# Split weights kept in DRAM after the first block, position rows read from DRAM on ACT's queue: a decoder layer on one Trainium2 core

## The chip, the cores and the metric

The kernel runs on one core of a Trainium2 chip. The metric is the device time of one launch in microseconds (us), lower is better. Its engines are TensorE (PE, with its weight loads shown apart as PEld), VectorE (DVE), ScalarE (ACT), GpSimd (POOL) and SyncE (SP), which only issues transfers here. SP and ACT each have a queue of their own for DMA transfers; both queues share the core's 16 DMA engines.

## What is computed

One decoder layer over 2048 tokens with a model width of 1024, all in float32. A combined projection feeds two branches, a gated DeltaNet (4 heads of 128) and a sliding-window attention (8 query heads of 64, 2 key/value heads, window 128) with a relative-position bias, which are gated and merged; a SwiGLU block with 2816 hidden columns follows.

```python
h = rms_norm(x, attn_norm[l])
proj = h @ w_in[l]
dn_qkv, dn_z, dn_b, dn_a, sq, sk, sv, gate_raw = split_combined(proj)
y_dn = gated_deltanet_branch(dn_qkv, dn_z, dn_b, dn_a, ...)
y_swa = sliding_window_branch(sq, sk, sv, q_gain, k_gain, sinks, rel_bias)
gates = sigmoid(gate_raw).reshape(B, S, 2, D_MODEL)
merged = gates[:, :, 0] * (y_dn @ w_branch_dn[l]) + gates[:, :, 1] * (y_swa @ w_branch_swa[l])
x = x + merged @ w_out[l]
h2 = rms_norm(x, ffn_norm[l])
x = x + (silu(h2 @ w_gate[l]) * (h2 @ w_up[l])) @ w_down[l]
```

In the attention branch `logits = where(mask, q k^T + bias, -inf)`, where `bias[head, i, j]` is a value of `rel_bias` (32 buckets by 8 heads) chosen by the distance between the query and the key.

## The kernel before

**Tiling.** The 2048 tokens are worked on in four blocks of 512. Each block goes through the same stages: the projections of keys and values (skv) and queries (sq), the DeltaNet projections and heads (dn) among which the attention tiles are spread, the branch gates (g), the branch outputs (br), their merge, the output product (wo), the norm, and the FFN in five parts of up and down products. The window products (skv, sq) of the next block are done before the FFN of this one.

**Weights.** They lie in DRAM as 120 units: two for skv (128 x 1056 values) and 118 others (128 x 1024, 512 KB each). Every block uses every unit once, so there are 480 loads. `weights()` (L151) loads a unit on SP's queue into `wraw` (three buffers) and splits it in two halves j = 0, 1. ACT copies the half to `whi`, rounded to the matmul's format fp32r; DVE and POOL in turn subtract (`wlo` = `wraw` - `whi`). `whi` and `wlo` have four half buffers each (HB). A product is then three matmuls (`mm3`, `tok_mm`): hi by hi, hi by the lo of the other operand, lo by hi. One unit is 24 matmuls of 512 columns. In `chan_gemm` (per-channel products: dn, g, br, up) the first half serves the first 12 of them and the second half the rest; in `tok_gemm` (wo, down) and in sq both halves are used in turn until the unit ends.

**Position bias.** `band_bias()` (L279) is a side task at the start of block 0. It loads the table and a one-hot matrix, multiplies them on PE (oh by rb), copies the 8 x 384 result to `tab`, and then needs, for each head, 128 rows that are each shifted by one against the last (`bt`). Eight transfers on SP's queue read them from the one SBUF partition that holds the head's row, 128 overlapping pieces of 1 KB each. Four pairs of heads are then flipped by a matmul with `anti` and copied to `bias`.

**Order.** PE runs in the order in which the program writes it. `drive()` (L193) mixes the dense products with side tasks (norms, attention tiles, DeltaNet heads, the bias): each side task says by its `yield` when it wants to go on, and an estimate of the engines' times (`Estimate`, L56) decides when it does. `weights()` uses the raw engine handles, so the estimate doesn't see the loads and the splits. The other engines run in an order that the scheduler sets from dependencies and priorities; side tasks have a higher priority. A queue's transfers and an engine's instructions start in their order; one that waits holds those behind it.

**Names.** `x` is a 128 x 512 half tile of the input; `xn` or the scaled `x` its normed form, `st` the norm's statistics, `h` the transposed pair (hi, lo). `kr`, `ksq`, `kst`, `kn` are steps of the key norm, `ba` the columns for beta and decay. `G` are the gates and then the merged branch, `mt` their split form. `be`, `bm`, `bl`, `bc`, `bch` and `B` belong to the DeltaNet heads. `acc` and `aux` are PSUM tiles. L108 in the rows is a line of a helper through which nearly every instruction passes.

Of the kernel before, what the change touches and what calls it, by code (L numbers as in the profile page):

```python
# [8 lines left out]
F32 = mybir.dt.float32  # L9
F32R = mybir.dt.float32r  # L10
I32 = mybir.dt.int32
AF = mybir.ActivationFunctionType
ALU = mybir.AluOpType
AX = mybir.AxisListType

P = 128
# [7 lines left out]
NQ = 8  # L24
# [3 lines left out]
FSPLIT = (4, 4, 4, 4, 6)  # L28
NU = 63
ND = 6  # L30
HB = 4
PSUB = 2
LANES = 2
GATES_AT = 2
# [18 lines left out]
UNITS = {k: i for i, k in enumerate(KEYS)}  # L53


class Estimate:  # L56


    def __init__(self):
        self.now = 0.0  # L60
        self.done = 0.0
        self.free = {}
        self.ready = {}
        self.banks = {}
        self.seq = 0
# [48 lines left out]
class Emitter:  # L114
    def __init__(self, ctx, tc, ins, out, nblocks):
        self.tc, self.raw, self.out = tc, tc.nc, out
        self.est = Estimate()
        self.nc = Noted(tc.nc, self.est)
        self.__dict__.update(ins)
        self.nblocks = nblocks  # L120
        pool = lambda name, bufs, **kw: ctx.enter_context(tc.tile_pool(name=name, bufs=bufs, **kw))
        self.cp = pool("const", 1)
        self.tp = pool("tiny", 2)
        self.wp = pool("w", 3)
        self.up = pool("u", NU)
        self.dp = pool("d", ND)
        self.bp = pool("b", 1)
        self.pacc = pool("acc", 8, space=bass.MemoryType.PSUM)
        self.nsub = 0

# [20 lines left out]
    def weights(self, key, a):  # L151
        nc = self.raw
        n = a * 264 if key[0] == "skv" else 1024
        src = self.w_skv[key[1]] if key[0] == "skv" else self.w_all[UNITS[key]]
        raw = self.wp.tile([P, 1056], F32, name="wraw", tag="wraw")
        nc.sync.dma_start(out=raw[:, :n], in_=src)
        hl = []
        for j in range(2):
            hi = self.wp.tile([P, 528], F32R, name="whi", tag="whi", bufs=HB)
            lo = self.wp.tile([P, 528], F32R, name="wlo", tag="wlo", bufs=HB)  # L160
            r = raw[:, j * n // 2:(j + 1) * n // 2]
            nc.scalar.activation(hi[:, :n // 2], r, AF.Copy)  # L162
            self.nsub += 1
            eng = nc.vector if self.nsub > 6 and self.nsub % PSUB else nc.gpsimd
            eng.tensor_tensor(out=lo[:, :n // 2], in0=r, in1=hi[:, :n // 2], op=ALU.subtract)  # L165
            hl.append([t[:, :n // 2].rearrange("p (a m) -> p a m", a=a // 2) for t in (hi, lo)])
        h = a // 2
        return lambda k: (hl[k // h][0][:, k % h], hl[k // h][1][:, k % h])

    def mm3(self, ps, lh, ll, rh, rl, first, last):  # L170
# [108 lines left out]
    def band_bias(self):  # L279

        nc = self.nc
        yield 20000
        rb = self.u([8], name="rb")
        nc.sync.dma_start(out=rb[0:33, :], in_=self.rel_bias)
        oh = self.u([384], name="oh")
        nc.sync.dma_start(out=oh[0:33, :], in_=self.onehot)
        anti = self.u([P], name="anti")
        nc.sync.dma_start(out=anti, in_=self.flip)
        yield 8000
        ps = self.aux()  # L290
        nc.tensor.matmul(ps[0:8, 0:384], rb[0:33, :], oh[0:33, :], start=True, stop=True)
        tab = self.u([384], name="tab")
        nc.vector.tensor_copy(out=tab[0:8, :], in_=ps[0:8, 0:384])
        bt = [self.u([2, 2 * P], name="bt") for _ in range(4)]
        for h in range(NQ):
            row = tab[h:h + 1, :]
            src = bass.AP(tensor=row.tensor, offset=row.offset, ap=[list(row.ap[0]), [1, P], [1, 2 * P]])
            nc.sync.dma_start(out=bt[h // 2][:, h % 2, :], in_=src)
        yield 0
        yield 14000  # L300
        for i in range(4):
            ps = self.aux()
            nc.tensor.matmul(ps, anti, bt[i], start=True, stop=True)
            nc.scalar.activation(self.bias[:, 2 * i:2 * i + 2, :], ps, AF.Copy)
            yield 0
        self.bias_ready = True
# [775 lines left out]
```

## Time and profile before

| | us |
|---|---|
| median of 3 runs | 3273.05 (3271.22 to 3273.44) |
| the profiled execution, its own time | 3272.67 |
| its span, first to last instruction | 3270.9 |
| PE busy | 3122.2 (95% of the span) |
| DVE busy | 1752.7 (54%) |
| ACT busy | 1262.6 (39%) |
| POOL busy | 896.7 (27%) |

The mean granted clock of PE is 0.982 of full speed. The four blocks end at roughly 930, 1733, 2536 and 3271 us. Of the engines other than PE, ACT spends 604.0 us and POOL 640.5 us on splitting weights, DVE 356.4. The transfers move 281.27 MB, a mean of 86 GB/s.

A row of the timeline gives the start, the duration, the engine, the line, the operation, its output and inputs, and how many alike stand in a row; in square brackets stands how long the engine sat idle before it and which instruction released it.

### The profile page before, as it was taken

The numbers are of one execution on the slowest core, as the hardware profiler recorded it, in microseconds if no ns is written. First come the engines' busy times: TensorE is split into PE (matmuls) and PEld (weight loads), VectorE is DVE, ScalarE is ACT, GpSimd is POOL, SyncE is SP. The second block draws the span as 40 slices with busy tenths as digits, with TensorE's granted clock in tenths as the row PEclk, the third lists the DMA queues.
The fourth block names the chain that finished last, engine by engine and source line by source line (L and its number), as shares of the span: only waits on it lengthen the run. The fifth ranks groups of instructions, "written<-read, shape, count | busy, mean of one in ns | idle before, by whom it ended". The sixth has DMA issues, their size and how long they took to land. (4 is left out here: it accounts for less than half of the span.)

```text
span 3270.9 us, 40889 instructions
## 1 busy us (share of the span) xinstructions
PE 3122.2 (95%) x14854; PEld 2536.8 (78%) x14854; DVE 1752.7 (54%) x3986; ACT 1262.6 (39%) x2832; POOL 896.7 (27%) x761
## 2 busy tenths in 40 slices
PE   4899999999999999999999999999999899999999
PEld 3777878788877787778887777877888788878887
DVE  4776756633356765653337586555333757643333
ACT  3445335532334444542233444354222344332222
POOL 1433222422232322242223232133222422212222
PEclk8999999999999999999999999999999999999999
DMA  5221232233232223223332123322333212323332
GB/s 98 71 65 46 69 120 77 71 97 96 91 107 67 65 91 109 71 78 97 94 105 92 59 69 99 98 77 84 93 94 113 80 59 68 107 84 91 97 97 90
DMA packets 84674, 281.27 MB, mean 86 GB/s; under 512 B 9431, under 2 KB 10616, under 8 KB 84472
## 3 DMA queue, kind: packets, MB, share of 16 engines
q1 hardware_dynamic: 71800, 255.59, 26.6%
q10 hardware_dynamic: 12672, 23.07, 2.0%
q8 instruction: 116, 1.90, 0.2%
q14 instruction: 86, 0.70, 0.1%
HBM read 269.19 MB, written 8.39 MB: 85 GB/s over the span
## 5 line engine op out<-in xcount | busy, mean ns | idle before, releaser
L108 PE MATMUL acc<-h,whi 128*128 128x512 f32 x4864 | 1555.4, 401 | 3.0 <-DVE kd L108 2.5
L165 POOL TENSOR_TENSOR wlo<-wraw,whi 128x512 fp32r<-128x512 f32 (+1 forms) x483 | 640.5, 1327 | 2167.0 <-ACT whi L162 2113.2
L162 ACT ACTIVATE whi<-wraw 128x512 fp32r<-128x512 f32 (+1 forms) x960 | 604.0, 632 | 1327.8 <-PE acc L108 1111.8
L108 PEld LDWEIGHTS acc<-h,whi 128*128 128x128 f32 x4864 | 906.2, 190 | 201.6 <-issue 7.0
L108 PE MATMUL acc<-h,wlo 128*128 128x512 f32 x2432 | 963.9, 396 | 21.0 <-DVE wlo L165 20.1
L165 DVE TENSOR_TENSOR wlo<-wraw,whi 128x512 fp32r<-128x512 f32 x477 | 356.4, 748 | 563.6 <-ACT whi L162 490.0
L108 PEld LDWEIGHTS acc<-h,wlo 128*128 128x128 f32 x2432 | 461.8, 190 | 133.9 <-DVE wlo L165 22.7
L108 PE MATMUL acc<-whi,a 128*128 128x512 f32 x1408 | 442.0, 395 | 0.0
L108 PEld LDWEIGHTS acc<-whi,a 128*128 128x128 f32 x1408 | 263.3, 188 | 61.9
L108 PE MATMUL acc<-wlo,a 128*128 128x512 f32 x704 | 277.3, 394 | 0.0
L108 DVE TENSOR_TENSOR x<-x,acc 128x512 f32<-128x512 f32 x192 | 131.5, 686 | 112.5 <-PE acc L108 112.4
L108 DVE SCALAR_TENSOR_TENSOR th<-th,acc 128x512 f32<-128x512 f32 x88 | 60.5, 688 | 194.6 <-ACT th L108 194.6
L108 PE MATMUL acc<-whi,mt 128*128 128x512 f32 x512 | 161.0, 396 | 0.5 <-DVE h L108 0.5
L108 PEld LDWEIGHTS acc<-wlo,a 128*128 128x128 f32 x704 | 132.6, 188 | 31.0
L108 DVE SCALAR_TENSOR_TENSOR cv<-xr,cst_sb,cv 128x512 f32<-128x512 f32 x144 | 124.5, 865 | 52.5 <-ACT cv L108 41.9
L108 PE MATMUL acc<-whi,h 128*128 128x264 f32 (+1 forms) x512 | 129.5, 345 | 0.0
L108 DVE TENSOR_TENSOR th<-th,acc 128x512 f32<-128x512 f32 x88 | 60.5, 687 | 124.0 <-PE acc L108 123.7
L108 DVE SCALAR_TENSOR_TENSOR a<-th,a 128x512 fp32r<-128x512 f32 x88 | 86.6, 984 | 69.0 <-ACT a L108 55.3
L108 PEld LDWEIGHTS acc<-whi,mt 128*128 128x128 f32 x512 | 95.8, 188 | 23.6 <-DVE h L108 0.9
L108 PE MATMUL acc<-wlo,mt 128*128 128x512 f32 x256 | 100.8, 394 | 0.0
L108 ACT ACTIVATE L<-L,ast 128x256 f32<-128x256 f32 (+1 forms) x192 | 83.3, 456 | 36.1 <-DVE ast L108 36.1
L108 PEld LDWEIGHTS acc<-whi,h 128*128 128x128 f32 x512 | 87.8, 191 | 11.2 <-issue 0.6
(195 smaller groups left out, 3516.7 us busy)
## 6 DMA issues: line engine op xcount, KB each, us to landing
wraw<-in_w_all SPq DMA_DIRECT2D x472, 512.0 KB, 3.6
x<-in_x ACTq DMA_DIRECT2D x56, 256.0 KB, 4.5
out<-x ACTq DMA_DIRECT2D x32, 256.0 KB, 3.7
wraw<-in_w_skv SPq DMA_DIRECT2D x8, 528.0 KB, 3.7
x<-in_x SPq DMA_DIRECT2D x8, 256.0 KB, 6.2
bt<-tab SPq DMA_DIRECT2D x8, 128.0 KB, 16.4
cst_sb<-in_cst SPq DMA_DIRECT2D x1, 497.5 KB, 5.8
anti<-in_flip SPq DMA_DIRECT2D x1, 64.0 KB, 5.4
```

Of the source, the lines that this page charges most:

```text
L108: r = f(*args, **kw)
L162: nc.scalar.activation(hi[:, :n // 2], r, AF.Copy)
L165: eng.tensor_tensor(out=lo[:, :n // 2], in0=r, in1=hi[:, :n // 2], op=ALU.subtract)
```

## The change

The change has two parts.

*Weights.* hi and lo of a half unit become one tile `whl` (128 x 2 x 528) with five buffers (WB); `wraw` has two (WR). In block 0 a unit is loaded and split as before, by the same three engines, and each half is then stored to DRAM (`wk`, 512 KB) on SP's queue. In blocks 1 to 3 the unit's two halves are loaded from there on SP's queue, 512 KB each, and nothing is split.

*Position rows.* The three constants are loaded on ACT's queue. The 8 x 384 table is stored to DRAM (`kept`), and four transfers on ACT's queue read the overlapping rows of two heads each from there. The task asks for its first matmul later (12000 for 8000).

```diff
--- before.py
+++ after.py
@@ -28,7 +28,8 @@
 FSPLIT = (4, 4, 4, 4, 6)
 NU = 63
 ND = 6
-HB = 4
+WR = 2
+WB = 5
 PSUB = 2
 LANES = 2
 GATES_AT = 2
@@ -125,6 +126,8 @@
         self.up = pool("u", NU)
         self.dp = pool("d", ND)
         self.bp = pool("b", 1)
+        self.kp = pool("kept", 1, space=bass.MemoryType.DRAM)
+        self.kept = {}
         self.pacc = pool("acc", 8, space=bass.MemoryType.PSUM)
         self.nsub = 0
 
@@ -151,20 +154,32 @@
     def weights(self, key, a):
         nc = self.raw
         n = a * 264 if key[0] == "skv" else 1024
-        src = self.w_skv[key[1]] if key[0] == "skv" else self.w_all[UNITS[key]]
-        raw = self.wp.tile([P, 1056], F32, name="wraw", tag="wraw")
-        nc.sync.dma_start(out=raw[:, :n], in_=src)
+        h = a // 2
         hl = []
-        for j in range(2):
-            hi = self.wp.tile([P, 528], F32R, name="whi", tag="whi", bufs=HB)
-            lo = self.wp.tile([P, 528], F32R, name="wlo", tag="wlo", bufs=HB)
-            r = raw[:, j * n // 2:(j + 1) * n // 2]
-            nc.scalar.activation(hi[:, :n // 2], r, AF.Copy)
-            self.nsub += 1
-            eng = nc.vector if self.nsub > 6 and self.nsub % PSUB else nc.gpsimd
-            eng.tensor_tensor(out=lo[:, :n // 2], in0=r, in1=hi[:, :n // 2], op=ALU.subtract)
-            hl.append([t[:, :n // 2].rearrange("p (a m) -> p a m", a=a // 2) for t in (hi, lo)])
-        h = a // 2
+        if key not in self.kept:
+            src = self.w_skv[key[1]] if key[0] == "skv" else self.w_all[UNITS[key]]
+            raw = self.wp.tile([P, 1056], F32, name="wraw", tag="wraw", bufs=WR)
+            nc.sync.dma_start(out=raw[:, :n], in_=src)
+            keep = []
+            for j in range(2):
+                t = self.wp.tile([P, 2, 528], F32R, name="whl", tag="whl", bufs=WB)
+                r = raw[:, j * n // 2:(j + 1) * n // 2]
+                hi, lo = t[:, 0, :n // 2], t[:, 1, :n // 2]
+                nc.scalar.activation(hi, r, AF.Copy)
+                self.nsub += 1
+                eng = nc.vector if self.nsub > 6 and self.nsub % PSUB else nc.gpsimd
+                eng.tensor_tensor(out=lo, in0=r, in1=hi, op=ALU.subtract)
+                if self.nblocks > 1:
+                    d = self.kp.tile([P, 2, n // 2], F32, name="wk", tag="wk%d_%d" % (len(self.kept), j))
+                    nc.sync.dma_start(out=d, in_=t[:, :, :n // 2].bitcast(F32))
+                    keep.append(d)
+                hl.append([t[:, e, :n // 2].rearrange("p (a m) -> p a m", a=h) for e in range(2)])
+            self.kept[key] = keep
+        else:
+            for j in range(2):
+                t = self.wp.tile([P, 2, 528], F32R, name="whl", tag="whl", bufs=WB)
+                nc.sync.dma_start(out=t[:, :, :n // 2].bitcast(F32), in_=self.kept[key][j])
+                hl.append([t[:, e, :n // 2].rearrange("p (a m) -> p a m", a=h) for e in range(2)])
         return lambda k: (hl[k // h][0][:, k % h], hl[k // h][1][:, k % h])
 
     def mm3(self, ps, lh, ll, rh, rl, first, last):
@@ -281,21 +296,22 @@
         nc = self.nc
         yield 20000
         rb = self.u([8], name="rb")
-        nc.sync.dma_start(out=rb[0:33, :], in_=self.rel_bias)
+        nc.scalar.dma_start(out=rb[0:33, :], in_=self.rel_bias)
         oh = self.u([384], name="oh")
-        nc.sync.dma_start(out=oh[0:33, :], in_=self.onehot)
+        nc.scalar.dma_start(out=oh[0:33, :], in_=self.onehot)
         anti = self.u([P], name="anti")
-        nc.sync.dma_start(out=anti, in_=self.flip)
-        yield 8000
+        nc.scalar.dma_start(out=anti, in_=self.flip)
+        yield 12000
         ps = self.aux()
         nc.tensor.matmul(ps[0:8, 0:384], rb[0:33, :], oh[0:33, :], start=True, stop=True)
         tab = self.u([384], name="tab")
         nc.vector.tensor_copy(out=tab[0:8, :], in_=ps[0:8, 0:384])
+        kept = self.kp.tile([8, 384], F32, name="kept", tag="kept")
+        nc.scalar.dma_start(out=kept, in_=tab[0:8, :])
         bt = [self.u([2, 2 * P], name="bt") for _ in range(4)]
-        for h in range(NQ):
-            row = tab[h:h + 1, :]
-            src = bass.AP(tensor=row.tensor, offset=row.offset, ap=[list(row.ap[0]), [1, P], [1, 2 * P]])
-            nc.sync.dma_start(out=bt[h // 2][:, h % 2, :], in_=src)
+        for i in range(4):
+            rows = bass.AP(tensor=kept.tensor, offset=kept.offset + i * 768, ap=[[1, P], [384, 2], [1, 2 * P]])
+            nc.scalar.dma_start(out=bt[i], in_=rows)
         yield 0
         yield 14000
         for i in range(4):
```

Some places show what this does to the order. First PE at the start of block 0: `whi_481` and `whl_487` are query weights, `bt` by `anti` the bias matmuls, `cst_sb` by `kn` the transposes of the normed keys. Before:

```order
L108 MATMUL acc_442<-whi_485,h_223 128x512
L108 MATMUL acc_442<-wlo_486,h_222 128x512
L108 MATMUL aux_501<-bt_322,anti_188 128x512
L108 MATMUL aux_504<-bt_323,anti_188 128x512
L108 MATMUL aux_507<-bt_324,anti_188 128x512
L108 MATMUL aux_510<-bt_325,anti_188 128x512
L108 MATMUL aux_513<-cst_sb_80,kn_435 128x128 x4
L108 MATMUL aux_522<-cst_sb_80,kn_438 128x128 x4
L108 MATMUL acc_443<-whi_481,h_213 128x512
```

On the same engine and place, after:

```order
L109 MATMUL aux_515<-cst_sb_82,kn_439 128x128 x4
L109 MATMUL aux_524<-cst_sb_82,kn_442 128x128 x4
L109 MATMUL acc_448<-whl_487,h_215 128x512
L109 MATMUL acc_448<-whl_487,h_216 128x512
L109 MATMUL acc_448<-whl_487,h_215 128x512
L109 MATMUL acc_448<-whl_492,h_224 128x512
L109 MATMUL acc_448<-whl_492,h_225 128x512
L109 MATMUL acc_448<-whl_492,h_224 128x512
L109 MATMUL acc_445<-whl_571,h_233 128x512
L109 MATMUL acc_445<-whl_571,h_234 128x512
L109 MATMUL acc_445<-whl_571,h_233 128x512
L109 MATMUL aux_584<-bt_376,anti_190 128x512
```

The transposes of kn now stand behind 42 query matmuls (36 matmuls and the four bias matmuls before), and the four bias matmuls behind nine more.

ACT at the same place, before:

```order
L108 ACTIVATE ba_406<-acc_268 128x8
L108 ACTIVATE kr_404<-acc_268 128x128
L108 ACTIVATE ba_406<-acc_269 128x8
L108 ACTIVATE kr_404<-acc_269 128x128
L108 ACTIVATE ba_406<-acc_270 128x8
L108 ACTIVATE kr_404<-acc_270 128x128
L162 ACTIVATE whi_485<-wraw_479 128x512
L108 ACTIVATE ba_406<-acc_271 128x8
L108 ACTIVATE kr_404<-acc_271 128x128
L108 ACTIVATE be_531<-ba_406 128x16
L108 ACTIVATE ksq_419<-kr_404 128x512
```

And after:

```order
L310 DMA kept_374<-tab_372 8x384 [waits DVE_49]
L109 ACTIVATE ba_410<-acc_270 128x8 [waits PE_49]
L109 ACTIVATE ba_410<-acc_271 128x8 [waits PE_49]
L109 ACTIVATE ba_410<-acc_272 128x8 [waits PE_49]
L109 ACTIVATE ba_410<-acc_273 128x8 [waits PE_49]
L314 DMA bt_376<-kept_374 128x2x256 [waits DMAHW7_49]
L314 DMA bt_377<-kept_374 128x2x256
L314 DMA bt_378<-kept_374 128x2x256 [waits DMAHW5_49]
L314 DMA bt_379<-kept_374 128x2x256 [waits DMAHW6_49]
L109 ACTIVATE kr_408<-acc_270 128x128
L109 ACTIVATE kr_408<-acc_271 128x128
L109 ACTIVATE kr_408<-acc_272 128x128
```

The store of the table and the four loads of rows now stand among ACT's own work; the first load waits for a transfer (DMAHW7, the store of the table), and the four kr with ksq stand behind it.

SP in block 0, after (before, there is one `wraw` load a unit and nothing else):

```order
L162 DMA wraw_1015<-in_w_all 128x1024
L174 DMA wk_869<-whl_866 256x1x512
L174 DMA wk_874<-whl_871 256x1x512
L162 DMA wraw_1059<-in_w_all 128x1024
L174 DMA wk_1020<-whl_1017 256x1x512
L174 DMA wk_1025<-whl_1022 256x1x512
L162 DMA wraw_1124<-in_w_all 128x1024
L174 DMA wk_1064<-whl_1061 256x1x512
L174 DMA wk_1069<-whl_1066 256x1x512
```

A unit's raw load stands behind the two stores of the unit before the last. In blocks 1 to 3 only loads of `whl` from `wk` stand there, each of which waits for PE to have done with the buffer.

DVE at the end of the merge in block 1, where `x` (of block 2) is scaled by its norm. Before:

```order
L108 SCALAR_TENSOR_TENSOR G_10089<-G_10089,acc_10711 128x512
L108 SCALAR_TENSOR_TENSOR st1_10571<-st1_10571 128x4
L108 TENSOR_TENSOR G_10089<-G_10089,G_10090 128x512
L108 TENSOR_SCALAR x_10474<-x_10474,st1_10571 128x512
L108 TENSOR_SCALAR x_10505<-x_10505,st1_10571 128x512
```

And after:

```order
L109 TENSOR_SCALAR x_10462<-x_10462,st1_10547 128x512
L109 TENSOR_SCALAR x_10487<-x_10487,st1_10547 128x512
L109 TENSOR_SCALAR x_10497<-x_10497,st1_10547 128x512
L109 TENSOR_SCALAR x_10520<-x_10520,st1_10547 128x512
L109 TENSOR_SCALAR x_10463<-x_10463,st1_10547 128x512
L109 TENSOR_SCALAR x_10488<-x_10488,st1_10547 128x512
L109 TENSOR_SCALAR x_10498<-x_10498,st1_10547 128x512
L109 TENSOR_SCALAR x_10521<-x_10521,st1_10547 128x512
L109 SCALAR_TENSOR_TENSOR mt_10649<-G_9867,mt_10648 128x512
L109 SCALAR_TENSOR_TENSOR G_9985<-G_9985,acc_10656 128x512
L109 SCALAR_TENSOR_TENSOR G_10113<-G_10113,acc_10675 128x512
```

`G_10089` before and `G_10113` after belong to the last of the eight merges. The eight scalings stood behind it and now stand ahead of the last two.

## Rows read from the trace of the kernel before

**Rows 1.** Windows of one block: length, busy us of engines, PEclk, DMA share, GB/s.

```profile
0.00:930.00 930.00, 852.91 (x4104) 688.12 (x4105) 515.35 (x1286) 375.39 (x888) 261.03 (x223) 0.97 0.30 84
930.00:1733.00 803.00, 778.45 (x3724) 633.63 (x3723) 436.96 (x989) 315.59 (x707) 224.59 (x190) 0.99 0.29 88
1733.00:2536.00 803.00, 779.22 (x3719) 635.04 (x3718) 436.16 (x987) 315.24 (x706) 223.85 (x190) 0.99 0.29 87
2536.00:3271.00 735.00, 711.65 (x3313) 580.01 (x3311) 364.19 (x725) 256.40 (x532) 187.24 (x160) 0.99 0.28 85
```

**Rows 2.** Waits of PE, whole run: us in total, times, longest us.

```profile
PE aux L108 <- DVE x L108: 33.0, 7, 12.4
PE acc L108 <- DVE wlo L165: 20.1, 6, 4.8
PE aux L108 <- DMA bt<-tab: 19.3, 3, 8.0
...
PE aux L108 <- DVE xn L108: 5.9, 1, 5.9
```

**Rows 3.** Timeline of PE at the position rows: start, us, instruction, idle before.

```profile
49.58 1.02 PE L108 MATMUL aux<-bt,anti 128*128 128x512 f32 x2
56.14 2.05 PE L108 MATMUL aux<-bt,anti 128*128 128x512 f32 x2 [5.54 <-DMA bt<-tab]
...
75.87 1.91 PE L108 MATMUL aux<-cst_sb,kn 128*128 128x128 f32 x8
```

**Rows 4.** Timelines of DVE and ACT at the same place.

```profile
33.95 0.55 DVE L108 COPY tab<-aux 8x384 f32<-8x384 f32 x1 [3.32 <-PE aux L108]
...
47.20 2.52 DVE L108 TENSOR_TENSOR kn<-kr,kst 128x256 f32<-128x256 f32 x4
...
42.27 0.63 ACT L108 ACTIVATE ksq<-kr 128x512 f32<-128x512 f32 x1
```

**Rows 5.** Waits of PE in block 1 (930 to 1733 us).

```profile
PE aux L108 <- DVE x L108: 5.1, 1, 5.1
PE acc L108 <- DVE wlo L165: 4.8, 1, 4.8
...
PE aux L108 <- DVE be L108: 2.3, 3, 1.3
...
PE aux L108 <- POOL be L108: 1.5, 2, 1.3
```

**Rows 6.** Short windows: behind the wlo stall, at the x stall, the start, FFN.

```profile
1006.00:1012.00 6.00, 6.00 (x20) 4.80 (x20) 0.78 (x2) 1.23 (x2) 0.00 (x0) 0.58 0.52 178
1244.00:1252.00 8.00, 7.60 (x37) 6.78 (x38) 8.00 (x16) 5.32 (x8) 0.00 (x0) 0.63 0.49 168
1.75:12.00 10.25, 0.00 (x0) 0.00 (x0) 3.04 (x25) 4.82 (x17) 0.00 (x0) 1.00 0.96 341
640.00:910.00 270.00, 270.00 (x1167) 217.83 (x1166) 92.37 (x127) 80.26 (x133) 67.82 (x52) 1.00 0.31 95
```

**Rows 7.** The chain of waits, its last long piece.

```profile
2900.07 366.90 PE acc L108 x1584
```

**Rows 8.** Landing of wraw; issue (ns) and landing of out; the page's bt line.

```profile
DMA to landing us min/median/max: 3.2/3.6/12.7
...
L979 ACTq DMA_DIRECT2D out<-x x32: 338/338/529, 909.7 to 3267.7; - x32
...
DMA to landing us min/median/max: 2.0/3.7/6.2
...
bt<-tab SPq DMA_DIRECT2D x8, 128.0 KB, 16.4
```

**Rows 9.** Timeline of DVE and POOL in block 1: bm beside bl, and alone.

```profile
964.93 1.77 DVE L108 TENSOR_TENSOR bm<-B,cst_sb 128x512 f32<-128x512 f32 x1
...
964.42 3.43 POOL L108 TENSOR_TENSOR bl<-B,cst_sb 128x512 f32<-128x512 f32 x2 [3.19 <-DVE B L108]
...
996.86 0.69 DVE L108 TENSOR_TENSOR bm<-B,cst_sb 128x512 f32<-128x512 f32 x1
```

## The prediction

> **What bounds the kernel now.** I read the windows by stage first. TensorE (PE) is busy 852.91 of 930 us in block 0 and the next three windows of one block each leave 24.55, 23.78 and 23.35 us idle [rows 1]. With block 0's 77.09 that is 149 us of PE idle time, and the rest is matmul. The tail of the chain of waits gives the pace: 1584 matmuls of 512 columns in 366.90 us [rows 7], 231.6 ns each, so a weight unit (24 of them) takes 5.56 us and a half unit 2.78. In 640 to 910 us PE has no idle time at all while ACT, DVE and POOL are all splitting weights [rows 6]. The split is therefore hidden in dense stages, and taking it off ACT, DVE and POOL is worth nothing there. What can be won is only idle time and clock. The waits of PE name it: 19.3 us for the position rows (bt), 33.0 for x (most of it at the start), 20.1 for the low halves of weights (wlo), 5.9 for xn [rows 2]. In a middle block x and wlo cost one stall each, 5.1 and 4.8 us, and the be chain 2.3 + 1.5 [rows 5].
>
> A stall also costs clock. In the 6 us after the wlo stall PE is busy throughout and the granted clock is 0.58, near the lower of its two levels; around the x stall it is 0.63 over 8 us [rows 6]. That is 6 x 0.42 = 2.5 us and 8 x 0.37 = 3.0 us of work lost behind the stalls. Over a block the mean clock is 0.99 of 803 us [rows 1], some 8 us lost.
>
> **Part A, position rows (start of block 0).** Before, eight loads, each from a single partition, take 16.4 us to land in the median [rows 8]. PE starts the first bias matmuls at 49.58 and ends the kn transposes behind them at 75.87 + 1.91 = 77.78 [rows 3]. In these 28.2 us the work is four pairs at 1.02 (the first pair's time; the second pair, after the wait, took 2.05) and about 1.0 for kn at full clock: 5.1. So 23.1 us go if the loads are early. After, the order puts bt behind six more query matmuls, kn and nine more matmuls. When would it land? The copy of the table stood at 33.95 [rows 4]; its matmul moves 36 short matmuls back (264 columns, 0.12 us each by the pace above, 4.3 us), so the copy ends at 38.8. The store takes 3.7 (the median of the output stores [rows 8]) to 42.5, and ACT stands still for it, since the first bt load waits on ACT's own queue. Four issues, by the 338 ns of an output store's [rows 8], end at 43.9; bt is there by 48 if it lands as the output stores do. PE needs it near 55.7. So bt is no longer waited for. But kr and ksq queue on ACT behind that wait: four kr (an estimate of 0.3 us each, half of ksq's 0.63, which has four times the columns) put ksq at 45.1, where it was at 42.27 [rows 4], 2.9 us later. kn then ends at 49.7 + 2.9 = 52.6, and PE wants it at 49.58 + 6 x 0.23 = 51.0: a new stall of 1.6, with some clock 2. A = -23 + 2 = **-21 us**. Bounds: -24 if ACT is not held; -12 if the store takes 6.2 as the slowest output store did and bt still lands 16.4 us after its issue (over 60, near 5 us late, plus clock).
>
> **Part B, no split in blocks 1 to 3.** SP now brings hi and lo ready, so nothing on PE can wait for wlo: 4.8 + 2.5 = 7.3 us per block. The x stall: before, DVE scales x behind the last merge's two G operations, one matmul away from the transposes that need x; after, the order has the eight scalings ahead of the last two merges, whose matmuls (about 24, 5.6 us) then cover the 3.25 us that they take. I count it gone: 5.1 + 3.0 = 8.1. Block 3 has no next block's x; its stall is on xn (5.9), behind the norm of the whole block, where the split plays no part: it stays. The be chain on DVE and POOL is mixed with the subtractions, but has work of its own on POOL; half of 3.8 = 1.9, and 1.0 of clock. Of the other small waits (about 10 us of a block) a quarter, 2.5. So 20.8 in blocks 1 and 2, 12.4 in block 3: B = **-54 us**. Bounds: -22 (the wlo stalls alone, 3 x 7.3); -90 (nearly all idle time and clock).
>
> What becomes of freed DVE time is seen in one place: the bm product takes 0.69 us alone and 1.77 when POOL's bl product runs beside it [rows 9]. The Trainium skill ("SBUF — State Buffer", "SBUF: two separate sides") says that VectorE with two SBUF inputs and a GpSimd operation that reads SBUF take the shared port pair in turn, each holding it for its whole instruction. The trace agrees (1.77 is more than double). By that rule, with POOL's subtractions gone, all of be's wait and half of the small waits would go, 4.4 us a block or 13 in all, and the sum would be 3188; I stay with the half, since bl, the operation seen to hold DVE, stays on POOL.
>
> **Part C, the rest of block 0.** ACT, DVE and POOL split as before. New are two stores of 512 KB per unit on SP, and the read of unit n+2 stands behind both stores of unit n. A store waits for the subtraction, which runs ahead of PE by about 8 us (the buffers' depth, half a unit to two units), so SP's order is not late. The traffic is: 1.57 MB per unit in 5.56 us is 283 GB/s where units follow each other without a break, in 74 of block 0's 120 units (wo 8, FFN 66). At the start the queues moved 341 GB/s at a share of 0.96; the dense window moved 95 at 0.31, which scales to 306 at full share [rows 6]; block 0 as a whole 84 at 0.30, 280 [rows 1]. So 280 to 343 against 283: it just fits. C = **0** (from -5, DVE's order, to +10, by 280 GB/s and some waits).
>
> **Part D, weights read twice as large.** In blocks 1 to 3 a unit is two loads of 512 KB in 5.56 us, 188 GB/s, well under the above. The buffers are five halves. In per-channel products a half is reloaded four halves ahead, 11.1 us. In token products (sq, wo, down: 34 units a block) both halves are used until the unit ends, so the second half of unit n+2 can start only three matmuls before unit n ends and is needed three matmuls into n+2: 30 matmuls, 6.95 us. A 512 KB load lands in 3.2/3.6/12.7 us (min/median/max) [rows 8]; with two on the way perhaps 5. D = **+3** (0 to +20, for a few late ones with their clock).
>
> **Sum**, against the profiled execution's 3272.67 (span 3270.9; median of the runs 0.4 higher): 3272.67 - 21 - 54 + 0 + 3 = 3200.7, so **3201 us**. The bounds: 3272.67 - 12 - 22 + 10 + 20 = 3269 and 3272.67 - 24 - 90 - 5 = 3154.
>
> **Rivals.**
> 1. Block 0 becomes bound by DMA (slower). Reads and writes share the 16 engines and the three scalings above leave 0 to 20% of room; no row shows a mixture at this load. It decides from the point where a unit takes 6.55 us (1.57 MB at 240 GB/s): 1.0 us x 74 units = 73, which eats A + B. At 200 GB/s it is 7.86: 2.3 x 74 = +170, **3371**. Against it: the reads at the start reached 341.
> 2. Weight halves land late in token products (slower). At 8.5 us instead of under 6.95, each of 102 such units waits 1.55 us, +158: **3356**. For it: the slowest load took 12.7, and a store of 256 KB up to 6.2. Against it: the median of 3.6.
> 3. The stalls move instead of going. x waits on its own norm chain of some twenty small DVE operations, be on bl, as before; only A and the wlo stalls are won: 3272.67 - 21 - 22 + 3 = **3233** (3225 to 3266, with A at its lower bound and D high). For it: each chain stands a few us behind the stall that is removed, and I have no row of what is late next.
> 4. No difference: A eaten by new waits on ACT, B by D. Within 0.2% (6.5 us), **3273**.
>
> **How the numbers follow.** The forecast (up to 3225) has 0.60, of which 0.03 under 3165; rival 3 0.18; rival 4 0.05; rival 1 0.10; rival 2 0.07. So faster by over 0.2% 0.78, within 0.2% (about what a measurement of this kernel can tell from no change) 0.05, slower 0.17. The range from 3165 to 3275 leaves out the two slow rivals and the 0.03 below: 0.8 inside.
>
> **What would show it.** A: the wait on bt gone from PE's waits, a wait on kn of 1 to 3 us in its place, PE past kn before 55 us. B: no wlo in PE's waits, idle time of 10 to 14 us in the windows of each of blocks 1 to 3, mean clock over 0.99; x no longer a single 5 us wait at the end of the merge. C: block 0's FFN window still without idle time, DMA share near 0.9. D: landing of the halves under 6 us, and waits of PE on a DMA of under 1 us a block. It is wrong if PE waits on the halves or their DMAs in the FFN stages of block 0 (rival 1) or at every wo and down unit of the later blocks (rival 2), or if the idle time of blocks 1 and 2 stays at 18 us or more (rival 3).

## The result and the profile after

The changed kernel takes **3195.66 us** (median of 4 runs, 3194.42 to 3196.13) against 3273.23 before; the ratio is 0.9764 (95% interval 0.9747 to 0.9781). The forecast was 3201, its range 3165 to 3275.

The page, first the span and the engines, then the transfers:

```profile
span 3194.3 us, 39761 instructions
PE 3095.3 (97%) x14854; PEld 2523.6 (79%) x14854; DVE 1403.2 (44%) x3626; ACT 837.6 (26%) x2112; POOL 415.8 (13%) x401
whl<-wk SPq DMA_DIRECT2D x708, 512.0 KB, 3.9
wk<-whl SPq DMA_DIRECT2D x236, 512.0 KB, 3.5
wraw<-in_w_all SPq DMA_DIRECT2D x118, 512.0 KB, 5.0
```

The windows that answer to [rows 1], cut where each block ends now, then two stretches of block 0 (from shortly behind the kn transposes into the output product, and the dense FFN). Columns as there: length, busy us of PE, PEld, DVE, ACT, POOL, granted clock, DMA share, GB/s.

```profile
0.00:928.50 928.50, 856.23 (x4108) 692.35 (x4109) 503.10 (x1279) 366.03 (x872) 251.44 (x216) 0.97 0.64 223
928.50:1703.30 774.80, 767.39 (x3717) 627.47 (x3717) 319.78 (x867) 174.33 (x466) 62.22 (x69) 1.00 0.53 171
1703.30:2477.90 774.60, 767.40 (x3717) 627.52 (x3717) 320.14 (x867) 174.11 (x466) 62.16 (x69) 1.00 0.54 172
2477.90:3194.30 716.40, 704.28 (x3316) 576.27 (x3314) 260.14 (x613) 123.18 (x308) 39.99 (x47) 1.00 0.53 172
56.56:480.00 423.44, 380.30 (x1897) 307.15 (x1896) 282.86 (x722) 184.42 (x484) 127.73 (x109) 0.95 0.54 188
640.00:900.00 260.00, 260.00 (x1121) 209.33 (x1120) 83.09 (x123) 77.87 (x129) 61.98 (x49) 1.00 0.83 285
```

Blocks 1 to 3 are 28, 28 and 19 us shorter than in [rows 1] (27, 28 and 19 between the same matmuls, see the table below). Idle time of PE in block 1 fell from 24.55 to 7.41 us, and the clock is back at 1.00. But block 0 as a whole hardly gained, although the bias wait is gone. The same stretch of block 0 (an equal number of matmuls) took 404.34 us before:

```profile
80.66:485.00 404.34, 373.74 (x1898) 301.16 (x1897) 282.43 (x724) 185.11 (x485) 129.47 (x111) 0.97 0.24 74
```

It now takes 423.44, with 43.1 us idle for 30.6 and a clock of 0.95 for 0.97. What PE waits for there:

```profile
PE aux L109 <- DVE vb L109: 6.2, 2, 5.6
PE aux L109 <- DVE O L109: 5.8, 1, 5.8
PE acc L109 <- DVE whl L171: 4.9, 2, 3.1
PE aux L109 <- ACT W L109: 4.3, 1, 4.3
PE aux L109 <- DVE kd L109: 4.0, 1, 4.0
PE aux L109 <- ACT T L109: 3.5, 1, 3.5
```

vb, W and T are steps of the DeltaNet heads. Before, W cost PE nothing there, and the other two little:

```profile
PE aux L108 <- ACT T L108: 0.7, 1, 0.7
PE aux L108 <- DVE vb L108: 0.6, 1, 0.6
```

Since PE's order is the same in all these kernels from shortly behind the kn transposes on, the start of one and the same matmul can be compared. The table gives the lead over the kernel before, in us, at five such matmuls (they stood at 81, 662, 928, 1729 and 2530 us before) and at the last one; the kernels of the next section are in it. The times and leads of this table alone count from each run's first matmul, which starts 12.4 us into the span before; so the first of the five stands some 15 us behind the kn transposes.

| kernel | kn done | dense FFN of block 0 | end block 0 | end 1 | end 2 | last matmul | median |
|---|---|---|---|---|---|---|---|
| changed kernel | 24.0 | 2.3 | 2.7 | 29.6 | 57.7 | 77.0 | 3195.7 |
| e1_head | 24.4 | 23.0 | 23.0 | 25.1 | 25.2 | 25.3 | 3247.2 |
| e2_weights | -7.1 | -23.0 | -22.5 | 6.4 | 34.5 | 53.8 | 3221.8 |
| e3_mixer_nostore | 24.4 | 14.7 | 15.1 | 43.6 | 71.9 | 91.3 | 3186.6 |
| e8_split_always | 23.7 | 13.3 | 13.4 | 20.6 | 28.2 | 34.3 | 3236.5 |
| e9_wb4 | 23.6 | 25.3 | 25.4 | 24.6 | 26.0 | 25.2 | 3250.0 |
| f2_late_store | 23.8 | 16.0 | 16.5 | 43.6 | 72.0 | 90.7 | 3182.5 |
| f3_wr3 | 21.2 | 15.3 | 15.7 | 42.9 | 69.7 | 87.5 | 3183.0 |
| f6_wb4_wr3 | 22.5 | 23.5 | 24.0 | 50.7 | 78.9 | 95.1 | 3175.3 |
| e4_dummy | 23.2 | -0.2 | -2.8 | -25.2 | -44.3 | -55.7 | 3325.9 |
| e10_double_store | 12.4 | -89.8 | -212.9 | -184.8 | -157.2 | -140.5 | 3411.4 |

So the changed kernel gains 24 at the head, loses 22 between kn and the dense FFN of block 0, loses nothing in the dense FFN, and gains 27, 28 and 19 in the later blocks.

### The profile page after: what moved, and what is told of

The parts are those of the page before. It is cut to its first block, busy times and chain, and to the rows that moved or that the text cites. A ratio compares the mean times of both kernels' runs of the same rounds, so it can differ in the third digit from the quotient of the medians.

```text
span 3194.3 us, 39761 instructions
## 1 busy us (share of the span) xinstructions
PE 3095.3 (97%) x14854; PEld 2523.6 (79%) x14854; DVE 1403.2 (44%) x3626; ACT 837.6 (26%) x2112; POOL 415.8 (13%) x401
## 5 line engine op out<-in xcount | busy, mean ns | idle before, releaser
L109 PE MATMUL acc<-h,whl 128*128 128x512 f32 x7296 | 1760.1, 397 | 7.5 <-DVE whl L171 4.9
L109 PEld LDWEIGHTS acc<-h,whl 128*128 128x128 f32 x7296 | 1357.6, 189 | 313.9 <-DVE whl L171 5.8
L109 PE MATMUL acc<-whl,a 128*128 128x512 f32 x2112 | 493.7, 393 | 0.0
L109 PEld LDWEIGHTS acc<-whl,a 128*128 128x128 f32 x2112 | 395.5, 188 | 90.3
L171 POOL TENSOR_TENSOR whl<-wraw,whl 128x512 fp32r<-128x512 f32 (+1 forms) x123 | 167.0, 1359 | 565.4 <-ACT whl L168 472.6
L168 ACT ACTIVATE whl<-wraw 128x512 fp32r<-128x512 f32 (+1 forms) x240 | 149.0, 630 | 290.3 <-PE acc L109 136.1
L109 PE MATMUL acc<-whl,mt 128*128 128x512 f32 x768 | 181.9, 398 | 8.1 <-DVE h L109 7.6
L109 PEld LDWEIGHTS acc<-whl,mt 128*128 128x128 f32 x768 | 145.9, 191 | 43.2 <-DVE h L109 8.5
L171 DVE TENSOR_TENSOR whl<-wraw,whl 128x512 fp32r<-128x512 f32 x117 | 89.8, 768 | 121.4 <-ACT whl L168 120.9
L109 PE MATMUL acc<-whl,h 128*128 128x264 f32 (+1 forms) x768 | 139.8, 341 | 0.0
L109 PEld LDWEIGHTS acc<-whl,h 128*128 128x128 f32 x768 | 118.0, 188 | 16.7 <-issue 1.1
```

The costliest lines, as they stand in the source:

```text
L109: r = f(*args, **kw)
L168: nc.scalar.activation(hi, r, AF.Copy)
L171: eng.tensor_tensor(out=lo, in0=r, in1=hi, op=ALU.subtract)
```

## The experiments

Three theories for the 22 us lost in block 0's mixer: 1, the stores; 2, the new buffers (two raw, five halves that hold hi and lo); 3, the engines beside PE ran ahead during the old bias wait, and the lead that this gave is now missing.

**The two parts apart.** The diff's last hunk is `band_bias`: e1_head is the kernel before with that hunk alone (and the DRAM pool that it needs), e2_weights the changed kernel without it.

> The kernel before with the position-row part of the change alone; weights as before. In the changed kernel PE is 24 us ahead of before when the kn transposes are done, and only 2 us ahead at 660 us: some 20 us are lost in the mixer of block 0. Theory 1 (the stores of split weights cost it) and theory 2 (fewer buffers for raw and split weights cost it) both expect the whole head gain to stay here: 24 us, 3249 us. Theory 3 (the engines beside PE ran ahead during the bias wait, and without that wait PE runs into their chains later) expects the gain to be given back in block 0 here too: 2 to 6 us in all, 3267 to 3271 us.

3247.22 us (ratio 0.9920, 0.9906 to 0.9935). The lead of 24.4 at kn stays to the end, 25.3 at the last matmul. Theory 3 is out.

> The changed kernel with the position rows as before (eight transfers on SP from one SBUF partition each); weights kept in DRAM. Theories 1 and 2: block 0 loses its 20 us against before, blocks 1 to 3 gain 74: 3273 + 20 - 74 = 3219 us. Theory 3: the bias wait is back and with it the lead of the other engines, so block 0 is as before: 3273 - 74 = 3199 us. In both the waits of PE on bt are near 19 us; if the raw loads on SP now stand between or behind them, more.

3221.83 us (0.9845, 0.9828 to 0.9861), as theories 1 and 2 had it. The two parts add: 25.5 + 50.9 = 76.4 us, and both together gained 77.6. With the old transfers, bt still costs PE 20.2 us of waiting, and 6.0 on bias come to it:

```profile
PE aux L109 <- DMA bt<-tab: 20.2, 3, 8.5
PE aux L109 <- ACT bias L109: 6.0, 1, 6.0
```

**Stores left out.** In e3_mixer_nostore the dn, g, br, wo and down units aren't stored.

```diff
-                if self.nblocks > 1:
+                if key[0] in ("skv", "sq", "up"):
...
+            kept = self.kept[key] or self.kept[("up", UNITS[key] % NF, UNITS[key] // NF % 2)]
```

> The changed kernel without the stores of the dn, g, br, wo and down units: only skv, sq and up units are stored, and the later blocks read an up unit's halves in place of the others (so the later blocks compute with wrong weights; bytes, transfers and matmuls of blocks 1 to 3 are the same). Block 0's mixer then has no stores. Theory 1: the 20 us of the mixer come back, 3176 us. Theories 2 and 3: no change, 3192 to 3198 us.

3186.55 us (3181.31 to 3191.48). 12 of the 22 us come back (14.7 of lead for 2.3), not 20. The leads are those of the profiled execution, which took 3181.31; by the medians 9 us come back.

**No kept weights at all, new buffers.** e8_split_always loads and splits in every block, without stores.

```diff
-        if key not in self.kept:
+        if True:
...
-                if self.nblocks > 1:
+                if False:
```

> The changed kernel without stores and without kept weights: every block loads and splits as block 0 does, with two raw buffers and five half buffers; position rows from DRAM. Theory 2: block 0 ends where it does in the changed kernel (928 us), and the later blocks lose some 20 us each against before as well: 3273 - 3 + 60 = 3330 us; with blocks 1 to 3 as before 3270. Theory 1: block 0 is 24 us faster than before, blocks 1 to 3 as before: 3249 us. Theory 3: 3268 us.

3236.53 us, faster than e1_head, which no theory had. In block 0 it loses 10 us between kn and the FFN (23.7 to 13.3), so 10 of the 22 are the buffers' and 12 the stores'. In blocks 1 to 3 it gains 7.2, 7.6 and 6.1 although it splits. e9_wb4 is the same with four half buffers:

```diff
-WB = 5
+WB = 4
```

> The kernel that splits in every block, with four half buffers in place of five (each still holds hi and lo; two raw buffers). With five, its blocks 1 to 3 were 7.2, 7.6 and 6.1 us faster than with the buffers of before, and PE's wait on low halves (4.8 us a block) was gone there. If the fifth half buffer does that, blocks 1 to 3 go back by some 20 us here: 3255 us. If it is the pairing of hi and lo in one buffer or the order that came with it, 3237 us.

3249.99 us. Both effects go: block 0 keeps its 25, and blocks 1 to 3 are as before. So the fifth half buffer does both. PE's waits in block 1, first with five, then with four:

```profile
PE aux L109 <- DVE be L109: 5.0, 3, 1.9
PE aux L109 <- DVE x L109: 3.9, 1, 3.9
...
PE aux L109 <- ACT T L109: 2.2, 1, 2.2
```

```profile
PE aux L109 <- DVE x L109: 5.0, 1, 5.0
PE acc L109 <- DVE whl L171: 4.8, 1, 4.8
PE aux L109 <- DVE be L109: 2.9, 3, 1.9
```

With five the splits come early enough for PE (no wait on whl), but stand among the chain of the heads (T is new). In block 0 the second weighs more: T there costs 5.9 with five and 1.8 with four. That the place of the splits is what delays T is read from these waits; no run shows it by itself.

**How the stores cost 12 us.** ACT's waits for its splits between 57 and 480 us, in the changed kernel, then without the mixer's stores:

```profile
ACT whl L168 <- DMA wraw<-in_w_all: 25.5, 7, 8.5
...
ACT whl L168 <- DMA wk<-whl: 6.4, 1, 6.4
```

```profile
ACT whl L168 <- DMA wraw<-in_w_all: 6.0, 3, 3.4
```

Before there was none of these. (ACT idles another 21.9 us ahead of its splits for which the profile names no releaser, 6.7 without the mixer's stores and 8.9 before; the wait followed next is one of them.) SP itself waits for the subtractions, since a store needs the finished half; its waits in the same stretch of the changed kernel:

```profile
SPq L174 <- POOL whl L171: 182.6, 42, 13.8
SPq L174 <- DVE whl L171: 91.6, 26, 16.8
```

One such wait, followed from POOL and SP through ACT and DVE to PE (the changed kernel's timelines: start, us, instruction, idle before):

```profile
260.72 1.74 POOL L171 TENSOR_TENSOR whl<-wraw,whl 128x512 fp32r<-128x512 f32 x1
262.43 3.44 POOL L109 TENSOR_TENSOR pT<-pT,cst_sb 128x512 f32<-128x512 f32 x2
265.83 1.73 POOL L171 TENSOR_TENSOR whl<-wraw,whl 128x512 fp32r<-128x512 f32 x1
```

```profile
262.49 5.61 SPq L174 DMA_DIRECT2D wk<-whl  x3
268.19 1.44 SPq L162 DMA_DIRECT2D wraw<-in_w_all  x2
```

```profile
273.14 0.63 ACT L168 ACTIVATE whl<-wraw 128x512 fp32r<-128x512 f32 x1 [3.95 <-issue]
273.67 0.61 ACT L109 ACTIVATE th<-cv 128x512 f32<-128x512 f32 x1
```

```profile
274.41 0.69 DVE L109 SCALAR_TENSOR_TENSOR cv<-th,cv 128x512 f32<-128x512 f32 x1
275.01 0.60 DVE L109 SCALAR_TENSOR_TENSOR vb<-aux,eg,vb 128x128 f32<-128x128 f32 x2
```

```profile
275.67 0.79 PE L109 MATMUL aux<-vb,R 128*128 128x128 f32 x2 [5.61 <-DVE vb L109]
```

The raw load stands here behind the stores of two units, the last three of them in the first SP row. The first goes out as POOL's first subtraction ends, the second right behind it (an issue takes 0.52 us in the median). The third waits for POOL's second subtraction, which stands behind two products for the attention (pT) and ends at 267.56. The raw loads stand behind that store and go out at 268.19 and after, although the buffer of the first had been free since POOL's first subtraction ended at 262.46. ACT, which has the split next in its order, stands until 273.14 (a raw load lands in 5.1 us in the median here); th, which vb's place on DVE waits for, stands behind it; PE waits 5.61 us.

This is the longest delay of its kind. Set against the end of the subtraction that frees its buffer, the 47 raw loads between 57 and 480 us go out 0.65 us late in the median and 5.7 at most; in e3_mixer_nostore and e8_split_always it is 0.03 and 0.1. The order of the queue or the slower transfer could be the cause, so f2_late_store writes the stores of a unit one unit later (f4_late_wr3 the same with a third raw buffer, f3_wr3 the third raw buffer alone, both with `WR = 3` and `NU = 62`):

```diff
             nc.sync.dma_start(out=raw[:, :n], in_=src)
+            self.store_kept(1)
...
-                    nc.sync.dma_start(out=d, in_=t[:, :, :n // 2].bitcast(F32))
-                    keep.append(d)
+                    keep.append((d, t[:, :, :n // 2].bitcast(F32)))
...
+    def store_kept(self, leave):
+        while len(self.late) > leave:
+            for d, t in self.late.pop(0):
+                self.raw.sync.dma_start(out=d, in_=t)
```

> The changed kernel with each unit's stores written one unit later, so that on SP's queue the raw load of unit n+2 stands ahead of the second store of unit n. In the changed kernel ACT waits 25.5 us for raw loads in block 0's mixer, 6.0 without the mixer's stores, none before. Theory 1a (the order on SP's queue holds the raw loads back): some 6 of the 12 us that the stores cost come back, 3190 us. Theory 1b (the transfers are slower beside the stores: a raw load lands in 5.0 us, 3.6 without stores): nothing comes back, 3196 us.

3182.50 us (0.9725, 0.9711 to 0.9740): 13 us, all that the stores had cost, and more than the 6 expected. The bytes are the same, so it is the order on SP's queue and what it does to the lookahead; a raw load now goes out 0.03 us after its buffer is free in the median. The landing of raw loads in the mixer came down with it, from 5.1 to 4.2 us in the median; what each of the two gave is not separated. ACT's waits on raw loads fell only from 25.5 to 17.0 us, so not every one of them reaches PE.

> The changed kernel with three raw buffers for two (and 62 common buffers for 63, to make room). Theory 1 in either form ends in ACT waiting for raw loads; with one more unit of lookahead that wait goes, and with it most of the 20 us of block 0's mixer: 3178 to 3184 us. Theory 2 in its other form (what costs is the place of the splits among the DeltaNet chain on ACT, DVE and POOL, not the wait for raw loads): 3192 to 3200 us.

3183.01 us: one more raw load ahead does the same.

> Both together: late stores and three raw buffers. If raw loads are the cause, 3175 to 3180 us, no better than the third raw buffer alone by more than 4. If not, 3192 to 3200 us.

3182.52 us: both do no more. So theory 1a holds as far as this goes: loads that stand further ahead in the queue give the 12 us back, be it by their earlier issue or by their faster landing. The 10 us of theory 2 remain.

**The split's work in the later blocks.** e4_dummy does a split in blocks 1 to 3 whose result nobody reads, from the half just loaded.

```diff
+                r = t[:, 0, :n // 2].bitcast(F32)
+                hi = self.wp.tile([P, 528], F32R, name="dhi", tag="dhi", bufs=1)
+                nc.scalar.activation(hi[:, :n // 2], r, AF.Copy)
+                self.nsub += 1
+                eng = nc.vector if self.nsub % PSUB else nc.gpsimd
+                eng.tensor_tensor(out=hi[:, :n // 2], in0=r, in1=hi[:, :n // 2], op=ALU.subtract)
```

> The changed kernel in which blocks 1 to 3 do the work of the split all the same, on ACT and on DVE and POOL in turn, from the half just loaded into a scratch buffer that nothing reads; PE waits for the loads alone, as in the changed kernel. Without the split blocks 1 to 3 gained 20, 20 and 13 us (against the kernel that splits in every block, with the same buffers). Theory W (PE's wait on the low halves was the cost): little comes back, 3196 to 3206 us. Theory E (the work itself held the chains of the DeltaNet heads on ACT, DVE and POOL): most of the 53 comes back, 3230 to 3250 us.

3325.94 us, far beyond both. ACT's waits in block 1 say why:

```profile
ACT dhi L184 <- DMA whl<-wk: 268.3, 135, 6.7
ACT dhi L184 <- POOL dhi L187: 65.6, 44, 6.7
```

The dummy put ACT, in its order, behind 135 landings, and the heads' steps behind ACT. It measures that wait and not the work, so it doesn't tell W from E. The pair e8_split_always and changed kernel does, with equal buffers: with the split there was no wait on whl in block 1, and yet without it blocks 1 to 3 are 19.7, 20.5 and 13.2 us shorter. That speaks for E: the work stood in the way of the heads' chains. Whether by its place in the engines' order or by slowing DVE's other operations, no run separates.

**The margin of block 0's transfers.** e10_double_store stores each half twice.

```diff
+                    d2 = self.kp.tile([P, 2, n // 2], F32, name="wx", tag="wx%d_%d" % (len(self.kept), j))
+                    nc.sync.dma_start(out=d2, in_=t[:, :, :n // 2].bitcast(F32))
```

> The changed kernel with each half stored twice in block 0 (the second copy is not read). In its dense window the DMA engines moved 285 GB/s at a share of 0.83, 343 at full share. With two more stores a unit is 2.62 MB, 7.65 us at 343 GB/s against 5.56 of matmul, so 74 dense units lose 2.09 us each: +155, and the mixer, at 7.5 us of PE per unit, some 10 to 30 more: 3360 to 3380 us, with no idle-free window in block 0's FFN. If SP's issues bind first (five of about 0.5 to 1.1 us a unit), the time is in the same region or below, and the DMA share stays under 0.9. If neither binds, 3200 to 3220 us.

3411.42 us (ratio 1.0426), beyond the 3360 to 3380 expected. Its dense stretch and PE's wait there (700 to 1100 us):

```profile
750.00:1050.00 300.00, 240.45 (x895) 183.15 (x894) 75.34 (x97) 56.53 (x97) 54.70 (x37) 0.90 0.88 326
PE acc L109 <- ACT whl L168: 75.7, 24, 5.0
```

A thousand matmuls of that stretch took 336.2 us, so a unit 8.07: 2.62 MB at 325 GB/s, where 7.65 was expected. The DMA share of 0.88 stays under the 0.9 that was named for the case that SP's queue binds first, and SP waits 88 us of the 300 for subtractions, with raw loads behind them. So 325 GB/s is a rate that the DMA engines reached, not shown to be their limit. Between the table's first two matmuls it lost 102 us, 80 more than the changed kernel, where 10 to 30 more were expected (some 13 of it fall in the first dense units). In the mixer a raw load goes out 7.2 us after its buffer is free in the median.

**Buffers.** f5_wb6 is f2_late_store with six halves and 62 common buffers; f6_wb4_wr3 is f2_late_store with four halves and three raw buffers, the memory of before:

```diff
-WR = 2
-WB = 5
+WR = 3
+WB = 4
```

> The kernel with late stores, with six half buffers for five (and 62 common buffers for 63). With late stores block 0's mixer is 16.5 us ahead of before where the head alone is 23 ahead; the rest is waits of PE on ACT's T and DVE's vb, kd and O. If it is the splits' lookahead that puts these behind, a sixth buffer gives back some of the 7: 3175 to 3180 us. If it is the place the scheduler gives them, no change or either sign by 5: 3178 to 3188 us.

3182.13 us: no change, so lookahead isn't what is missing.

> The kernel with late stores, three raw buffers and four half buffers (the memory of before). With four half buffers and no stores block 0 was 25 us ahead of before, with five 13. If the fifth half buffer is what costs block 0's mixer its remaining 10 us, and a third raw buffer hides the stores, block 0 is 23 to 25 us ahead here. Blocks 1 to 3 need 27 matmuls (6.25 us) of cover for a load that lands in 3.9: as in the changed kernel, 74 us ahead: 3173 to 3177 us. If the gain of blocks 1 to 3 rested on the fifth buffer too (7 us a block when they split), 3190 to 3196 us. If stores bring the loss back with any buffers, 3182 us.

**3175.30 us** (5 runs, 3172.16 to 3177.03; ratio 0.9705, 0.9692 to 0.9719), the fastest: block 0 keeps 24.0, and blocks 1 and 2 gain 26.7 and 28.2 without the fifth buffer. Block 3 gains 16.2 for 19.3. Against the changed kernel three things differ (late stores, a third raw buffer, four halves); whether both of the first two are needed with four halves was not run. PE's waits on the loads, 903 to 2450 us, stay small:

```profile
PE acc L109 <- DMA whl<-wk: 0.9, 3, 0.4
```

## Why the prediction was right, and where its terms were off

**A, the position rows: -21 forecast, 24 measured at kn (25.3 as a kernel of its own).** The mechanism was as told; PE at the place of [rows 3], and ACT where [rows 4] had ksq at 42.27:

```profile
51.36 1.30 PE L109 MATMUL aux<-cst_sb,kn 128*128 128x128 f32 x8 [0.77 <-DVE kn L109]
...
54.57 3.59 PE L109 MATMUL aux<-bt,anti 128*128 128x512 f32 x8
...
38.38 0.28 ACTq L310 DMA_DIRECT2D kept<-tab  x1
...
40.94 2.63 ACTq L314 DMA_DIRECT2D bt<-kept  x4
...
44.43 0.63 ACT L109 ACTIVATE ksq<-kr 128x512 f32<-128x512 f32 x1
```

ksq is 2.2 us later than before (2.9 forecast), the new wait on kn 0.77 (1.6), all eight bias passes run without a stall. bt lands in 6.4 us in the median, not 3.7, but PE needs it 11 us after its issue. The forecast had ACT stand still for the store; it had the four ba to do meanwhile, and the first bt load went out 2.6 us after the store. What held kr were the four issues, 2.63 us for 1.35.

**B, the later blocks: -54 forecast, -74 measured.** The sizes are off, not the direction. wlo is gone from PE's waits, as told. The x stall in the merge is gone too; xn in block 3 stayed (4.6 of 5.9). The terms that were too small are the quarter of the small waits and the share of the clock: PE's waits of block 1 are now

```profile
PE acc L109 <- DVE h L109: 2.8, 1, 2.8
PE aux L109 <- DVE be L109: 2.1, 3, 0.9
PE aux L109 <- DVE h L109: 0.9, 1, 0.9
PE aux L109 <- DVE qT L109: 0.5, 1, 0.5
```

and 0.8 more. The small waits fell from 10.8 to 4.8 us, by 6.0 where 2.5 had been counted; those on be from 3.8 to 2.3, by 1.5 for 1.9. 17.1 us of idle time went in block 1 and 9.8 with the clock, where 14.3 (4.8 + 5.1 + 1.9 + 2.5) and 6.5 (2.5 + 3.0 + 1.0) had been counted. I had stayed with a half because bl on POOL still holds DVE (bm beside it takes 1.77 as in [rows 9]). But POOL's subtractions had held more of DVE's work than bl does. DVE's part of be in block 1, before and after (ns, min/median/max):

```profile
L108 DVE TENSOR_TENSOR be<-bch,cst_sb x4: 1080/1496/2370, 972.2 to 1148.7; 128x900 fp32r<-128x900 f32 x4
```

```profile
L109 DVE TENSOR_TENSOR be<-bch,cst_sb x4: 1078/1079/1082, 966.3 to 1128.0; 128x900 fp32r<-128x900 f32 x4
```

Of the two slow ones before, one (1909 ns) ran beside two subtractions on POOL, the other (2370) beside POOL's own part of be. Apart from the 90.2 us of subtractions, DVE's busy time in block 1 fell from 346 to 320 us for the same work. What DVE's operations took beyond the shortest of their kind (counted from 0.15 us up) was 41.4 us before, 30.8 of it in operations that ran beside a subtraction on POOL and 1.3 beside bl; it is 15.7 now.

So the rule of the Trainium skill that stood beside this term ("SBUF — State Buffer", "SBUF: two separate sides") described this kernel better than my half: by it the sum was 3188 with B at -67. What had been worked out from it holds for the small waits (6.0 of 10.8 us went), not for be's (1.5 of 3.8 went, not all); and no run shows how much of the gain comes from DVE's shorter operations and how much from the split's work being gone.

**C, the rest of block 0: 0 forecast, +22 measured, the term that was wrong.** It lies outside its bound of +10. The dense FFN was right: no idle time at a DMA share of 0.83 and 285 GB/s (0.31 and 95 in [rows 6]), and e10_double_store shows 325 GB/s with reads and writes mixed, 15% above the 283 that are needed; rival 1 would have needed under 240. The step that failed is "a store waits for the subtraction, which runs ahead of PE by about 8 us, so SP's order is not late". It asked whether the weights come in time for PE. They do as well as before (PE waits 6.2 us on halves in the stretch, 6.7 before). But the subtraction was not early for SP, which waited 182.6 us for POOL's and 91.6 for DVE's. Much of that costs nothing, since the same subtraction frees the raw buffer; what is new is the issue of the stores and, at times, a store that waits for POOL ahead of a raw load that could go. And ACT, which splits, also carries the heads' steps in one order, and a split that waits for its raw load holds these: 12 us. That the fifth half buffer costs block 0 another 10 us was not in the sum at all.

**D, the double bytes: +3 forecast.** Nearly nothing: the halves land in 3.9 us in the median (8.4 at most), and PE waits 0.5 us for one of them in the whole run. Rival 2 is out.

The total came out within 6 us since C's 22 and the 20 that B was short cancel; that is luck. Two slips in the working change nothing: block 3's share of B is 12.7, not 12.4 (7.3 + 1.9 + 1.0 + 2.5), and 341 GB/s at a share of 0.96 scales to 355, where C has 343. Rival 3 (the stalls move) is out for blocks 1 to 3, but names what happened in block 0.

## What to carry to other kernels

When work is taken off an engine that is never the bottleneck, count the waits of the bottleneck that end on that engine and on those whose operations it slows down, not the busy time: here about 27 us in a middle block, while the dense stages gained nothing. When a transfer is added ahead of a load in one queue, ask what the added transfer itself waits for, follow the load to the engine that consumes it, and ask what else stands behind that wait in the engine's order; one load issued earlier or one more buffer gave back 13 us. Buffers cut both ways where a scheduler fills the engines: a fifth half buffer saved 7 us a block in three blocks where they split (next to nothing where they don't) and cost 10 to 12 in one, so each size is worth a run of its own.

## What the runs showed of the hardware that was not expected

- Eight transfers of 128 KB, each from one SBUF partition, landed in 16.4 us in the median [rows 8]; four of 256 KB with the same overlapping 1 KB rows from DRAM landed in 6.0 to 6.7.
- Reads and writes mixed moved 326 GB/s at a DMA share of 0.88 in e10_double_store; the reads alone at the start had moved 341 at 0.96 [rows 6]. The mixture cost little here.
- Stores to DRAM of 512 KB landed in 3.5 us in the median and the loads of raw weights beside them in 5.0; the loads had taken 3.6 before [rows 8].
